# One decoder layer on one core: loads, tiles and transposes of the projection stage arranged in another way

## The chip, the core and the metric

The kernel runs on one core of a Trainium2 chip. Times are device microseconds (us) of one execution. The engines are PE (TensorE, matmuls and transposes), ACT (ScalarE), DVE (VectorE), POOL (GpSimd) and SP, which here only issues DMAs. Each engine runs its instructions in their order and waits on semaphores for the others.

## What is computed

One layer over 2048 tokens of width 1024, float32 in and out. The products are made in three parts of higher and lower halves, so that each float32 product of 128 tokens with a 1024 x 512 weight is 24 matmuls (3 terms, 8 blocks of k).

```python
a = _rmsnorm(h, g_in)                       # rows of x
q, k, v, gate_b, u_a, v_a, gate_a = split(a @ w_in)
q = _rope(_rmsnorm(q, q_norm), positions)   # 8 heads of 64
k = _rope(_rmsnorm(k, k_norm), positions)
o_b = _dilated_attention(q, k, v) * silu(gate_b)   # windows (128,1) (512,4) (2048,16)
o_a = _gmlp_spatial(u_a, v_a, w_spatial, b_spatial, ln_v_g, ln_v_b) * silu(gate_a)
h = h + concat(o_b, o_a) @ w_out
h = h + sigmoid(_rmsnorm(h, g_ple) @ w_ple_gate + b_ple_gate) * (p @ w_ple_proj)
```

## The kernel before

The work has three stages. In the first, 16 tiles of 128 tokens are scaled (`norm_T`, L206), turned so that the width lies on the partitions, and multiplied with the weights of gate_b (g), q, k and v (`project`, L227). A row tile is turned in one of two ways: the first `PE1` = 2 tiles by PE (`split_part`, L155), the others by the DMA (`turn_words`, L172): ACT takes the 32-bit words apart into two planes of 16 bits (L179), SP issues a DMA transpose for each (L181), DVE copies the planes back together (L183, two copies). `split_words` then makes the high part on ACT (L193) and the low part on DVE (L194), which PE reads as `aT`.

The four weights arrive in pieces of 256 KB on SP's queue (`load_group`, L127); ACT makes a high part (L133), Pool or DVE a low part (L135). The four small tables (positions `pos_i`, frequencies `freq`, `q_norm` and `k_norm` in `nrm`) and the broadcast of g_in to 128 partitions (`gbc`, L274, 512 KB) are loaded on SP's queue as well, gbc ahead of the weights and the others behind the first of them.

For each of q and k `post_qk` (L402) squares on ACT (L405), reduces (L407), rotates with tables `ta`, `tb` (L413, L415, sum on Pool L114), raises the sum of squares to the power -1/2 on Pool (L148, the scale before it on DVE L147), multiplies (L420) and splits in halves `hl` (ACT L422, DVE L423). `turn_qk` (L426) turns these with one DMA transpose `st<-hl` (L429), reorders k's result on ACT (L432) and stores it (L435). `post_gb` (L449) evacuates gate_b on ACT (L451) and DVE (L452) and stores it.

The loop over tiles has the order q, k, v, g of the tile before, while `prep(n)` makes the next one ready. A scheduler of the framework orders the instructions of each engine by priority in that loop; from attention on, PE's order is written out by hand (`in_order`). Buffers for pieces and turned words come from one ring of four, `stage()`, whose tiles are called raw.

In the second stage, attention works on 4 head pairs x 3 dilations in steps of four blocks; scores (L755) are followed after one step by the softmax (L758 to L766) and the splitting and turning of the probabilities (`Step.turn`, L769 to L781, `pt<-raw`), and after six steps by values (L791). gMLP products (L627) stand between as fill: `BLOCK0` = 18 units ahead of the first step, 1.3 per step after that. k and q of a head pair are loaded by `load_qk` (L257 to L266) into one set of buffers `sq` and `sk` by pieces, in the last steps of the pair before. The third stage (w_out, gate) has no part in the change.

## Time and profile before

| | |
|---|---|
| median of 3 runs | 1290.81 us (1289.02 to 1296.98) |
| the profiled execution | 1295.01 us, its span 1293.2 us |
| mean granted clock of PE | 0.976 |
| PE busy | 1201.3 us, 93% |
| DVE, ACT, POOL busy | 888.2, 648.9, 512.1 us |

PE is busy for nine tenths of the span, and the chain that ended last goes mostly through PE. Times in the profile are counted from the start of the span. An entry such as `[1.72 <-DVE gb L452]` behind a row says that the engine stood idle for 1.72 us before it and that DVE's instruction of line 452 on tile gb released it. A name such as `aT<-xt` is the tile written and the tile read. "x8" joins eight instructions that follow one another.

### The profile page before, as it was taken

Reading aid. Unit: us, or ns where it says so; the run is one execution under the profiler, and the core shown is the slowest. Engines: PE = TensorE matmul, PEld = TensorE weight load, DVE = VectorE, ACT = ScalarE, POOL = GpSimd, SP = SyncE. Lnnn points to the kernel's source line nnn. Section 1 sums busy time; section 2 is a strip of 40 time slices with the busy share of each in tenths; the row PEclk is TensorE's granted clock in tenths of the full one; section 3 lists DMA queues with packets and bytes.
Section 4 is the critical chain, followed back from the end, with each engine's and each line's share of the span. In section 5 each row is a group of like instructions: output and inputs, shape, how many; then the busy total and the mean of one; then the engine's idle time right before and its main releaser. Section 6 shows DMA issues by size and latency. Waiting matters only on the chain.

```text
span 1293.2 us, 21329 instructions
## 1 busy us (share of the span) xinstructions
PE 1201.3 (93%) x7166; PEld 976.0 (75%) x7166; DVE 888.2 (69%) x2253; ACT 648.9 (50%) x1273; POOL 512.1 (40%) x454
## 2 busy tenths in 40 slices
PE   5999999989995799899799799879999999999998
PEld 4778877767884687687687688768778888888887
DVE  5885565655575678778778678598766766666733
ACT  5754334334344577677677677444334434434422
POOL 4852343433453456555555565342212121221100
PEclk9999999999997899899999999989999999999999
DMA  7598777776769899999999999955555655654531
GB/s 263 160 229 197 168 183 166 165 180 157 175 171 239 202 202 220 219 216 236 218 217 223 219 229 215 207 176 174 141 147 123 165 156 128 153 162 127 143 90 49
DMA packets 442254, 233.21 MB, mean 180 GB/s; under 512 B 337440, under 2 KB 392864, under 8 KB 442144
## 3 DMA queue, kind: packets, MB, share of 16 engines
q1 hardware_dynamic: 442144, 231.85, 75.4%
q8 instruction: 56, 0.92, 0.3%
q14 instruction: 54, 0.44, 0.1%
HBM read 102.66 MB, written 57.28 MB: 124 GB/s over the span
## 4 chain that ended last, share of the span: by engine, by line
PE 41%; DMA 19%; DVE 16%; ACT 7%; issue 7%; POOL 6%; SPq 4%; DVEq 0%; ACTq 0%; POOLq 0%
PE mm L227 17%; PE mm L627 8%; PE gt L227 5%; DMA pt<-raw 4%; DMA xt<-raw 3%; PE s L227 3%; DMA st<-hl 3%; PE s L755 3%; PE pt L791 2%; DVE aT L194 2%; DMA ob<-d_o 2%; ACT raw L179 2%; POOL rsh L148 2%; DVE m L420 1%; DVE pr L758 1%
## 5 line engine op out<-in xcount | busy, mean ns | idle before, releaser
L227 PE MATMUL mm<-wslot,aT 128*128 128x512 f32 x1536 | 362.8, 392 | 7.8 <-ACT aT L193 3.3
L227 PEld LDWEIGHTS mm<-wslot,aT 128*128 128x128 f32 x1536 | 289.4, 189 | 70.4 <-ACT aT L193 4.6
L627 PE MATMUL mm<-wslot,aT 128*128 128x512 f32 x1152 | 317.9, 418 | 23.2 <-DVE raw L618 14.2
L627 PEld LDWEIGHTS mm<-wslot,aT 128*128 128x128 f32 x1152 | 214.1, 197 | 63.5 <-DVE raw L618 14.6
L114 POOL TENSOR_TENSOR raw<-pr,raw 128x512 f16<-128x512 f32 (+1 forms) x152 | 178.0, 1177 | 151.6 <-ACT raw L773 137.9
L766 ACT ACTIVATE pr<-pr,ost 128x256 f32<-128x256 f32 (+1 forms) x384 | 150.5, 451 | 78.8 <-DVE ost L764 70.9
L227 PE MATMUL gt<-wslot,aT 128*128 128x512 f32 x744 | 177.8, 393 | 6.1 <-DVE gb L452 5.3
L227 PEld LDWEIGHTS gt<-wslot,aT 128*128 128x128 f32 x744 | 139.8, 189 | 38.0 <-DVE gb L452 7.0
L791 PEld LDWEIGHTS <-pt 128*128 128x128 f16 x1800 | 66.3, 99 | 62.1 <-issue 33.7
L773 ACT ACTIVATE raw<-pr 128x512 f16<-128x512 f32 (+1 forms) x152 | 93.2, 620 | 39.6 <-DMA pt<-raw 37.4
L791 PE MATMUL pt<-sv,pt 128*128 128x65 f16 x1800 | 83.6, 196 | 21.8 <-DMA pt<-raw 21.8
L758 DVE CUSTOM_DVE_ANT_0 pr<-s,mask 128x256 f32<-128x256 f32 (+1 forms) x256 | 81.3, 359 | 29.7 <-POOL raw L114 16.0
L227 PE MATMUL av<-wslot,aT 128*128 128x512 f32 x360 | 86.0, 392 | 7.3 <-DVE gb L452 6.3
L227 PE MATMUL s<-wslot,aT 128*128 128x512 f32 x384 | 90.0, 390 | 1.6 <-POOL wslot L135 1.6
L114 POOL TENSOR_TENSOR m<-m,m 128x512 f32<-128x512 f32 x32 | 47.9, 1498 | 94.8 <-DVE rsh L147 88.8
L227 PEld LDWEIGHTS av<-wslot,aT 128*128 128x128 f32 x360 | 67.2, 188 | 23.6 <-DVE gb L452 7.9
L227 PEld LDWEIGHTS s<-wslot,aT 128*128 128x128 f32 x384 | 72.0, 188 | 17.0 <-POOL wslot L135 2.0
L755 PEld LDWEIGHTS <-sq 128*128 128x128 f16 x768 | 70.4, 121 | 13.7 <-issue 7.4
L755 PE MATMUL s<-sk,sq 128*128 128x256 f16 (+1 forms) x512 | 73.7, 279 | 7.0 <-DMA sk<-d_k 6.1
L566 POOL TENSOR_TENSOR ma<-ob,ma 128x512 f32<-128x512 f32 x16 | 24.5, 1533 | 122.1 <-DMA ma<-d_gb 58.0
L563 POOL TENSOR_TENSOR ob<-ob 128x512 f32<-128x512 f32 x16 | 21.0, 1314 | 126.5 <-DVE ob L561 126.5
L764 DVE TENSOR_SCALAR ost<-ost 128x2 f32<-128x2 f32 (+1 forms) x152 | 66.9, 442 | 2.6
(209 smaller groups left out, 1723.4 us busy)
## 6 DMA issues: line engine op xcount, KB each, us to landing
xt<-x SPq DMA_DIRECT2D x32, 512.0 KB, 4.6
d_o<-ost SPq DMA_DIRECT2D x48, 264.0 KB, 3.2
raw<-w_in SPq DMA_DIRECT2D x38, 256.0 KB, 3.7
sv<-d_vt SPq DMA_DIRECT2D x32, 264.0 KB, 3.5
ob<-d_o SPq DMA_DIRECT2D x16, 528.0 KB, 4.6
xt<-d_at SPq DMA_DIRECT2D x16, 512.0 KB, 5.0
out<-th SPq DMA_DIRECT2D x32, 256.0 KB, 2.8
d_at<-raw SPq DMA_DIRECT2D x28, 256.0 KB, 2.5
```

The source lines that it names most:

```text
L114: nc.gpsimd.tensor_tensor(dst, a, b, op=op)
L148: nc.gpsimd.tensor_tensor(dst, dst, mhalf[:, :width], op=OP.pow)
L179: nc.scalar.activation(turned[t].bitcast(U16), words[:, t], AF.Copy)
L194: nc.vector.tensor_tensor(lo, f, hi.bitcast(F32), op=OP.subtract)
L227: nc.tensor.matmul(ps, aT[:, ha, k, :], w(slot, hw, k), start=(n == 0), stop=(n == 3 * nk - 1))
L627: nc.tensor.matmul(ps, GT[c][:, ha, k, :], slots[g][:, hw, k, :], start=(n == 0), stop=(n == 23))
L755: nc.tensor.matmul(ps[:, c:c + nk], cols(br, j, Q[h]), cols(br, j, K, n, h, self.nb), start=(n == 0), stop=(n == 1))
L758: nc.vector.tensor_tensor_reduce(pr[:, c:c + nk], ps[:, c:c + nk], mask[:, m - nk:m], -1.0, 3e38, op0=OP.add, op1=OP.min, accum_out=o[:, j ...
L764: nc.vector.tensor_scalar(nm, nm, math.log(PSCALE), None, op0=OP.add)
L766: nc.scalar.activation(pr[:, c:c + nk], pr[:, c:c + nk], AF.Exp, bias=o[:, j - j0, 130 + h:131 + h], scale=-1.0)
L773: nc.scalar.activation(ph, pr[:, :width], AF.Copy)
L791: nc.tensor.matmul(PO[0][:, j % 2, h], self.pt[:, t, c // 128], vt[:, h, vv, 0:65], start=(n == 0), stop=(n == 3 * self.nb - 1))
```

## The change

1. g_in is read as two rows of 512 on ACT's queue; PE multiplies each by a column of ones into PSUM and DVE copies the result to `gbc`. The second tile's x is loaded on ACT's queue, too. The four small tables are loaded on Pool's queue; the rotation tables are computed behind the scaling of tiles 0 to 2.
2. `PE1` is 3: three tiles are turned by PE and each of the first weights meets three tiles. The order of weights is g, k, q, v.
3. In the loop k stands ahead of q. The copy back of the next tile's turned words, its splitting, its stores and the next x load (`finish(rest)`) get a place behind `LAST`, the two instructions that make q's halves of the current tile.
4. The spatial weights are prepared at tile 3 and parked in DRAM (`d_ws`); `gm_constants` loads them. `post_gb` of the last two tiles takes its buffer from `stage()`; gelu of c = 0 no longer does.
5. q and k lie in DRAM in blocks of 512 tokens, and `load_qk` loads a quarter of a head pair at a time, in four steps instead of three, k in two DMAs of 256 KB.
6. `BLOCK0` is 11. A step of width 256 has one DMA transpose and no longer two.

```diff
-BLOCK0, FILL = 18, 1.3
+BLOCK0, FILL = 11, 1.3
-PE1, PE3 = 2, 2
+PE1, PE3 = 3, 2
-        nc.sync.dma_start(gbc, bcast(io["g_in"], D))
-        ORDER = "gqkv"
+        XT[1] = stream.tile([128, D], F32, name="xt")
+        for i, t in enumerate((sn, cs)):
+            row = t.rearrange("p n d -> p (n d)")[0:1, :]
+            nc.scalar.dma_start(row, io["g_in"][0:1, 512 * i:512 * i + 512])
+            ps = bank("mm")
+            nc.tensor.matmul(ps, ones[0:1, :], row, start=True, stop=True)
+            nc.vector.tensor_copy(gbc[:, 512 * i:512 * i + 512], ps)
+        nc.scalar.dma_start(XT[1], x_t[1])
+        ORDER = "gkqv"
-        nc.sync.dma_start(pos_i, io["positions"].rearrange("o (n p) -> p (o n)", p=128))
+        nc.gpsimd.dma_start(pos_i, io["positions"].rearrange("o (n p) -> p (o n)", p=128))
...
-        for i in range(2):
-            nc.vector.tensor_copy(turned[i].bitcast(U16).rearrange("p (k c t) -> p t k c", t=2, k=nk),
-                                  halves[:, :, i * nk:i * nk + nk])
+        def back():
+            for i in range(2):
+                nc.vector.tensor_copy(turned[i].bitcast(U16).rearrange("p (k c t) -> p t k c", t=2, k=nk),
+                                      halves[:, :, i * nk:i * nk + nk])
+        if rest is None:
+            back()
+        else:
+            rest.append(back)
...
+            LAST[:] = [nc.scalar.activation(hl[:, :, 0], r, AF.Copy).ins,
+                       nc.vector.tensor_tensor(hl[:, :, 1], r, hl[:, :, 0], op=OP.subtract).ins]
...
-            g = p1g.tile([128, 512], F32, name="gb")
+            g = p1g.tile([128, 512], F32, name="gb") if n < NT - 2 else stage()
...
+        def finish(rest):
+            with tc.issue_after(LAST[0]), tc.issue_after(LAST[1]):
+                for f in rest:
+                    f()
...
-            t = pool.tile([128, 512], F32, name=name, bufs=n) if c else stage()
+            t = pool.tile([128, 512], F32, name=name, bufs=n)
...
+            if n < NT - 1:
+                for g in "kq":
+                    step(n - 1, g)
+            finish(rest)
+            if n < NT - 1:
+                for g in "vg":
+                    step(n - 1, g)
...
-            for t in range(2):
-                nc.sync.dma_start(qk[1][i:i + 64, t, :, tl], d_qk[1][64 * t:64 * t + 64, 2 * hp:2 * hp + 2, tl])
+            nc.sync.dma_start(qk[1][i:i + 64, c].rearrange("p t h s -> p t (h s)"),
+                              bass.AP(tensor=src.tensor, offset=src.offset,
+                                      ap=[[4 * HEADS * 512, 64], [64 * 4 * HEADS * 512, 2], [1, 1024]]))
...
-                        h, c = {10: (1, 0), 11: (1, 1), 0: (0, 2)}.get(i % 12, (4, 0))
+                        h, c = {10: (1, 0), 11: (1, 1), 0: (0, 2), 1: (0, 3)}.get(i % 12, (4, 0))
```

The lines below stand as the built programs have them. First ACT in one steady tile of the projection stage, before: sq of q and of k (from banks mm and s), the high part of the next tile (L193), both hl, gb, and behind them the square of the tile after (L210), k's reordering (L432) and the words (L179).

```order
L405 ACTIVATE sq<-mm 128x512
L179 ACTIVATE raw<-raw 128x256 x4
L193 ACTIVATE aT<-raw 128x512
L405 ACTIVATE sq<-s 128x512
L193 ACTIVATE aT<-raw 128x512
L422 ACTIVATE hl<-m_1536 128x8x64
L442 ACTIVATE vt<-av,sv 128x8x64
L422 ACTIVATE hl<-m_1581 128x8x64
L451 ACTIVATE gb<-gt 128x512
L210 ACTIVATE aT,ss<-xt 128x1024
L432 ACTIVATE hl<-st 128x1024
L179 ACTIVATE raw<-xt 128x1024 x2
```

The same engine and place in the changed kernel (s is k's bank there, mm q's; L456 is k's reordering, L202 the high part of the next tile, L475 gb):

```order
L429 ACTIVATE sq<-s 128x512
L183 ACTIVATE raw<-raw 128x256 x2
L429 ACTIVATE sq<-mm 128x512
L446 ACTIVATE hl<-m_1938 128x8x64
L466 ACTIVATE vt<-av,sv 128x8x64
L456 ACTIVATE hl<-st 128x1024
L446 ACTIVATE hl<-m_1984 128x8x64
L475 ACTIVATE gb<-gt 128x512
L202 ACTIVATE aT<-raw 128x512 x2
L183 ACTIVATE raw<-xt 128x1024
```

The high parts of the next tile have moved from among the squares to behind gb, and k's reordering from behind gb to ahead of q's halves. DVE at the same place of the changed kernel (L444 the multiplication, L447 the low half, L188 the copies back, L476 gb, L203 the low part of the next tile):

```order
L437 TENSOR_TENSOR m_1793<-mm,ta 128x512
L439 TENSOR_TENSOR m_1794<-mm,tb 128x8x32 x2
L150 TENSOR_SCALAR rsh<-ssh 128x8
L444 TENSOR_TENSOR m_1747<-m_1747,rsh 128x512
L447 TENSOR_TENSOR hl<-m_1747,hl 128x8x64
L467 SCALAR_TENSOR_TENSOR vt<-gt,sv,vt 128x8x64
L444 TENSOR_TENSOR m_1793<-m_1793,rsh 128x512
L447 TENSOR_TENSOR hl<-m_1793,hl 128x8x64
L188 COPY raw<-xt 128x2x512 x2
L188 COPY raw<-raw 128x2x128 x4
L476 SCALAR_TENSOR_TENSOR gb<-gb,av 128x512
L203 TENSOR_TENSOR aT<-raw,aT 128x512 x2
```

q's rotation stands ahead of k's multiplication, and the copies back follow q's low half, where before they stood ahead of the reduction of k. SP's queue where the projections end, in the changed kernel (mask, wsT, lng, lnb are gMLP's constants, sq and sk the first head pair's q and k):

```order
L471 DMA d_vp<-vt 32x4x1056
L485 DMA mask<-c_mask 128x512
L485 DMA wsT<-d_ws 128x512
L485 DMA lng<-ln_v_g 128x512
L485 DMA lnb<-ln_v_b 128x512
L477 DMA d_gb<-raw 128x512
L273 DMA sq_3482<-d_q 128x512
L130 DMA raw<-w_in 128x512 x2
L477 DMA d_gb<-raw 128x512
L130 DMA raw<-w_in 128x512
L273 DMA sq_3483<-d_q 128x512
L277 DMA sk<-d_k 64x2x1024 x2
```

The program's records say that the sq load in this piece waits for PE's last projection matmul. The same weight loads in the kernel before, for which the first head pair's q and k come later:

```order
L435 DMA d_k<-hl 1024x1x128
L127 DMA raw<-w_in 128x512 x4
L429 DMA_TRANSPOSE st<-hl 128x8x128
L127 DMA raw<-w_in 128x512 x2
L435 DMA d_q<-st 1024x1x128
L127 DMA raw<-w_in 128x512 x2
L429 DMA_TRANSPOSE st<-hl 128x8x128
L127 DMA raw<-w_in 128x512
L435 DMA d_q<-st 1024x1x128
L127 DMA raw<-w_in 128x512 x2
```

They stood between the transposes and stores of the last two tiles, and now stand behind these.

## Rows read from the trace of the kernel before

**Rows 1.** The page's first line: span and instructions of the profiled execution.

```profile
span 1293.2 us, 21329 instructions
```

**Rows 2.** PE's timeline 0 to 95 us; columns: start, length, engine, line, operation, [idle before, releaser].

```profile
9.70 1.97 PE L155 MATMUL pt<-ident,xt 128*128 128x128 f32 x8 [9.70 <-DVE xt L216]
...
22.75 0.49 PE L227 MATMUL mm<-wslot,aT 128*128 128x512 f32 x1 [2.96 <-ACT wslot L133]
...
90.88 4.47 PE L227 MATMUL mm<-wslot,aT 128*128 128x512 f32 x19
```

**Rows 3.** SP's queue (it issues the loads), timeline 0 to 32 us.

```profile
10.32 4.32 SPq L303 DMA_DIRECT2D freq<-c_freq  x1
...
15.71 0.83 SPq L127 DMA_DIRECT2D m<-w_in  x2
```

**Rows 4.** DVE's timeline, one row at the start and two in the projections of tiles 6 and 14.

```profile
8.36 1.29 DVE L216 SCALAR_TENSOR_TENSOR xt<-xt,rs,gbc 128x1024 f32<-128x1024 f32 x1 [2.75 <-DMA gbc<-g_in]
...
162.32 1.26 DVE L147 TENSOR_SCALAR rsh<-ssh 128x8 f32<-128x8 f32 x1
...
368.67 1.78 DVE L420 TENSOR_TENSOR m<-m,rsh 128x512 f32<-128x512 f32 x1 [2.93 <-POOL rsh L148]
```

**Rows 5.** Pool's timeline 0 to 32 us.

```profile
5.68 0.56 POOL L148 TENSOR_TENSOR rs<-rs,mhalf 128x1 f32<-128x1 f32 x1 [5.24 <-DVE rs L147]
```

**Rows 6.** PE's timeline in the projections of tiles 6 and 14.

```profile
168.92 5.78 PE L227 MATMUL av<-wslot,aT 128*128 128x512 f32 x24 [1.72 <-DVE gb L452]
...
344.35 11.04 PE L227 MATMUL mm<-wslot,aT 128*128 128x512 f32 x48
```

**Rows 7.** DVE's groups by form; columns: operation, count | busy, mean ns | idle before.

```profile
L420 DVE TENSOR_TENSOR m<-m,rsh 128x512 f32<-128x512 f32 x32 | 26.5, 830 | 12.7 <-POOL rsh L148 12.6
...
L423 DVE TENSOR_TENSOR hl<-m,hl 128x512 f16<-128x512 f32 x32 | 22.6, 705 | 9.1 <-ACT hl L422 9.1
...
L183 DVE COPY raw<-xt 128x1024 uint16<-128x1024 uint16 x28 | 19.6, 751 | 31.9 <-DMA xt<-raw 29.7 <-issue 2.2
...
L147 DVE TENSOR_SCALAR rsh<-ssh 128x8 f32<-128x8 f32 x32 | 20.3, 635 | 0.0
```

**Rows 8.** Pool's groups by form, same columns.

```profile
L148 POOL TENSOR_TENSOR rsh<-rsh,mhalf 128x8 f32<-128x8 f32 x32 | 59.6, 1864 | 1.0 <-DVE rsh L147 0.7
...
L114 POOL TENSOR_TENSOR m<-m,m 128x512 f32<-128x512 f32 x32 | 47.9, 1498 | 94.8 <-DVE rsh L147 88.8 <-DVE m L415 5.4 <-ACT hl L422 0.5
```

**Rows 9.** ACT's groups by form, same columns.

```profile
L422 ACT ACTIVATE hl<-m 128x512 f16<-128x512 f32 x32 | 20.1, 629 | 82.9 <-DVE m L420 82.9
...
L432 ACT ACTIVATE hl<-st 128x1024 f16<-128x1024 f16 x16 | 17.8, 1113 | 37.9 <-DMA st<-hl 35.3 <-DVE xt L216 2.6
```

**Rows 10.** DMA issues of the whole run: count, size, median us to landing.

```profile
raw<-w_in SPq DMA_DIRECT2D x38, 256.0 KB, 3.7
...
st<-hl SPq DMA_TRANSPOSE x32, 3.4
```

**Rows 11.** PE's timeline 340 to 450 us, from projections to attention.

```profile
387.87 11.04 PE L627 MATMUL mm<-wslot,aT 128*128 128x512 f32 x48
...
413.10 7.19 PE L627 MATMUL mm<-wslot,aT 128*128 128x512 f32 x24 [14.19 <-DVE raw L618]
...
424.41 0.40 PE L755 MATMUL av<-sk,sq 128*128 128x128 f16 x4
...
442.14 0.61 PE L791 MATMUL pt<-sv,pt 128*128 128x65 f16 x6 [5.84 <-DMA pt<-raw]
```

**Rows 12.** SP's queue, timeline 345 to 410 us.

```profile
349.46 2.73 SPq L127 DMA_DIRECT2D raw<-w_in  x2
```

**Rows 13.** Busy time by window: window, length, then busy us and count of each engine.

```profile
500.00:550.00 50.00, 42.76 (x378) 32.84 (x376) 38.34 (x128) 33.22 (x69) 30.31 (x27) 0.90 1.08 219
```

**Rows 14.** The page's costliest groups: scores in attention.

```profile
L755 PE MATMUL s<-sk,sq 128*128 128x256 f16 (+1 forms) x512 | 73.7, 279 | 7.0 <-DMA sk<-d_k 6.1
```

**Rows 15.** PE's timeline 853 to 876 us.

```profile
854.21 13.89 PE L627 MATMUL mm<-wslot,aT 128*128 128x512 f32 x48 [4.49 <-DVE gv L618]
```

More of the change, by code (lines that the diff above doesn't have):

```diff
@@ L92, in hybrid_layer @@
     dram = ctx.enter_context(tc.tile_pool(name="dram", bufs=1, space=bass.MemoryType.DRAM))
-    d_qk = [dram.tile([128, HEADS, S], F16, name=f"d_{n}") for n in "qk"]
+    d_qk = [dram.tile([128, 4, HEADS, 512], F16, name=f"d_{n}") for n in "qk"]
+    d_ws = dram.tile([128, 512], F32, name="d_ws")
     d_vp = dram.tile([S, HEADS * 132], F16, name="d_vp")
@@ L466, in spatial_weights @@
-        def spatial_weights():
-            wsT, gg, bs = pg.tile([128, 4, 128], F32, name="wsT"), CG["gg"], CG["bs"]
-            CG["wsT"] = wsT
-            keep = stage()[:, 0:128]
-            nc.vector.tensor_scalar(keep, CG["mask"][:, 384:512], 0.0, None, op0=OP.is_ge)
-            pt = bank("pt", (128, 4, 128))
+            for name, src in (("mask", io["c_mask"]), ("wsT", d_ws),
+                              ("lng", bcast(io["ln_v_g"], 512)), ("lnb", bcast(io["ln_v_b"], 512))):
+                CG[name] = pg.tile([128, 512], F32, name=name)
+                nc.sync.dma_start(CG[name], src)
@@ L481, in step @@
+                nc.tensor.transpose(ps[:, g], w, ident)
+            nc.vector.tensor_copy(gg, ps.rearrange("p g s -> p (g s)"))
+            nc.sync.dma_start(d_ws, gg)
+            nc.vector.tensor_scalar(bs, bs, 0.25, None, op0=OP.mult)
         def step(n, g):
@@ L489, in step, with prep, store @@
                 (post_v if g == "v" else post_gb)(n, ps)
-        def prep(n):
-            if n < NT:
-                xt = XT.pop(n)
-                turned = None if n < PE1 else (stage(), stage())
-                AT[n] = norm_T(xt, xt, p1g if n % 3 == 2 else stream, turned, gbc)
+        def prep(n, rest=None):
+            xt = XT.pop(n)
+            turned = None if n < PE1 else (stage(), stage())
+            AT[n] = norm_T(xt, xt, p1g if n % 3 == 2 else stream, turned, gbc, rest)
+            def store():
                 if turned is None:
@@ L507, in turn_p @@
             nc.sync.dma_start(pp, io["p"][0, 0][n * 128:(n + 1) * 128])
-            turn_words(pp, two(turned))
-            nc.sync.dma_start(d_p[n], turned)
-        prep(0)
-        prep(1)
+            turn_words(pp, two(turned), rest)
+            rest.append(lambda: nc.sync.dma_start(d_p[n], turned))
+        def finish(rest):
+            with tc.issue_after(LAST[0]), tc.issue_after(LAST[1]):
+                for f in rest:
+                    f()
+        for n in range(3):
+            prep(n)
+        with tc.issue_after(scaled[1].ins):
+            gA, gB = angles()
+        for n in range(3):
+            tables(n)
         for c, g in enumerate(ORDER):
```

241 lines of the change are left out of this document (122 added, 119 removed).

## The prediction

> **What bounds the kernel now.** I read the span first: 1293.2 us of profile in an execution of 1295.01 us, so 1.8 us lie around it, and that execution is 4.2 us above the median of the three timed runs, 1290.81 [rows 1]. The sum below is made against 1295.0 and the 4.2 us come off at its end. TensorE (PE) is the engine that ends last in almost every stage, so the time of the kernel is PE's work plus PE's waits, and I looked for the waits by PE's timeline, stage by stage.
>
> *Start.* PE's transposes of tile 0 end at 11.7 us, its first projection follows, and tile 3's first one runs at 90.88. In between PE waits 2.96 us at 22.75 for weights [rows 2], because the next weight load is issued only at 15.71: ahead of it stand the small tables, of which the issue of freq alone holds the queue for 4.32 us [rows 3]. VectorE (DVE) scales tile 0 at 8.36 after 2.75 us of waiting for gbc, the broadcast of g_in [rows 4].
>
> *Tiles 3 to 13.* A tile is four products of 24 matmuls. Where PE waits for nothing, from 344.35 to 387.87, it does eight such products, 5.44 us each, so a tile is 21.76 us of PE [rows 6, 11]. At 168.92 PE waits 1.72 us for gb, the evacuation of a g product; eight tiles show such a wait, from 0.67 to 2.24 us; this row is one of them. From 90.88 to 344.35 are 11 tiles: 253.5 us, against 11 x 21.76 = 239.4 us of work. So 14.1 us are lost there [rows 2, 6].
>
> *From projections to attention.* The last projection ends at 387.87. PE goes on with gMLP products at once, stands still for 14.19 us, begins scores at 424.41 and, after a further wait of 5.84 us, the first values at 442.14, 54.3 us after the last projection [rows 11]. The weight pieces for this (24 of 256 KB) were issued from 349.46 on, beside the last projections [rows 12].
>
> *Attention.* From 500 to 550 us PE is busy 42.76 of 50 [rows 13]; 600 to 650 and 700 to 750, each round a change of head pair like it, are two more of this kind. Waits of scores for k's loads add up to 6.1 us [rows 14]. Near the end of attention PE waits 4.49 us for gMLP values [rows 15].
>
> **The change, part by part.**
>
> *A, start: -4 us.* g_in now comes by two small rows, two matmuls and two DVE copies. That takes DVE's wait of 2.75 us away, but two copies of 512 columns (0.7 each, as DVE's passes of that size [rows 7]) come in front of the scaling: I take 1.2 us earlier, g's first matmul at 10.5. From there to tile 3 stand 12 products, 65.3 us, and the transposes of tiles 1 and 2, 1.97 each by tile 0's row [rows 2], 3.9. With 1.6 us for weights (before 2.96 and some small waits) the twelfth product ends at 81.3. But tile 3 is the first that goes through the DMA, and its transposes now stand on SP's queue behind tile 2's q transpose and v's stores: 3.4 for landing, 0.75 copy, 0.63 for its high part, and two issues of 0.42 ahead of it make 5.6 us [rows 3, 7, 9, 10], so tile 3 starts at 86.9 instead of 90.88. Bounds: -9.6 if v's last products cover the stall, and from above rival 5.
>
> *Pool's issues: nothing.* Four loads stand on Pool's (GpSimd's) queue ahead of the power that gives tile 0's scale, which runs at 5.68 [rows 5]. No row of before shows what an issue costs Pool. SP's take 0.42 each (two weight loads in 0.83) to 4.32 (freq) [rows 3]: four of them are 1.7 to 17.3 us. As Pool has nothing else to do before 5.68, the first costs nothing, the second delays all by some 12 us. I take nothing, since Pool's queue is empty there, where SP's had ten loads under way; the upper end is a rival. The Trainium skill (page "SBUF — State Buffer", section "SBUF: two separate sides") speaks against this part: a load issued from Pool has its descriptors written by GpSimd, which is locked out of the port it shares with VectorE while that engine runs certain copies. [...] No run so far shows a load from Pool; in the row above DVE waits until 8.36, so by the rule, too, four prompt issues are through before DVE's long work begins.
>
> *B, tiles 3 to 13: +11.6 us.* Now k's product comes first and the copy back of the next tile's turned words is put behind q's high and low parts. PE's wait for gb goes: g's first four matmuls run early in the tile and gb is only needed a tile later. What comes in its place? On ScalarE (ACT) the next tile's high part stands behind gb of this tile, and that behind q's high part, and that behind L456, the reordering of k, which waits for k's DMA transpose. I walk that chain from a tile's first matmul. k's 24 matmuls are done after 34 matmuls, 7.7 us; square 0.6 (an ACT pass like L422's); three DVE passes of 0.7, to 10.4; Pool's addition 1.50 and power 1.86, to 13.8. Meanwhile q is done after 52 matmuls, 11.8; square, three passes and the scale (0.6 + 2.1 + 0.64) keep DVE until 15.1, so k's last multiplication (0.83) ends at 16.0; high part 0.63, low part 0.71, 17.3; transpose 3.4, 20.7; L456 1.11, 21.8; q's high and low part, 23.1; first copy back 0.75, high part of the next tile 0.63: 24.5 [rows 7 to 10]. Passes that follow one another on an engine overlap by nearly 0.1 us (48 matmuls are listed with 11.04 us, and 192 took 43.52, which is 10.88 for 48 [rows 6, 11]), and I take 0.4 off: a tile is 24.1 us, a wait of 2.3 for PE. 11 x 24.1 = 265.1, against 253.5 before. From below: the last g matmul at 21.76, then gb and the high part, 0.63 each, gives 23.0, thus -0.5 in all. From above: the scale at 1.26 and one multiplication at 1.78, both seen in this stage [rows 4], give 1.6 more, 25.7, thus +29. I take the walk, because each of its steps is a mean of 14 rows or more.
>
> *C, transition: +2 us.* The two last gb tiles and the weight pieces share one ring of four buffers, and on SP's queue the first load of q, into a buffer that is free only when the last projection has been read, stands ahead of all 24 pieces. So the loads that ran beside the last projections now begin after them. Four pieces at a time, 3.7 to land, 0.63 for the high part and up to 1.5 for the low part where Pool makes it, are 1.45 us a piece [rows 8, 9, 10]: 35 us, scores at about 35 us after the last projection (36.5 before). gelu of c = 0 no longer waits for a ring buffer and the transposes of the first steps no longer stand behind loads, so values follow 17.7 - 5.8 = 11.9 us later, at 47 instead of 54.3 us [rows 11]. But PE will have done 84 gMLP matmuls by then, not 118 (BLOCK0 is 11 and no longer 18): 34 x 0.227 = 7.7 us that come later. -7.3 + 7.7 is about nothing; as q's and k's loads stand between the pieces, I take +2. Bounds: the landing alone, 0.9 us a piece, gives -11; 2.0 us a piece, with as much time again for q's, k's and v's loads in between, gives +15.
>
> *D, attention: -6 us.* k and q come in quarters, a step or two sooner, with runs of 2 KB and not of 1 KB. That should take the 6.1 us of waits for k [rows 14]. Upper end: all idle time of the three stretches, 3 x 7.2 = 22 us [rows 13]; lower end nothing, since the same bytes go over the same queue.
>
> *E, end of attention: -2 us.* The 7.7 us of gMLP work that come later (C) fill part of the wait of 4.49 [rows 15]; bounds 0 and -4.5. The single transpose for narrow steps, three tables instead of two and the parking of d_ws are off PE's path: nothing, or one transpose group of 1 us ahead of tile 3, which waits anyway.
>
> **Sum.** -4 + 11.6 + 2 - 6 - 2 = +1.6: 1296.6 in an execution like the profiled one, 1292.4 against the median; I say 1292.
>
> **Rivals.**
> 1. *k's chain is longer still (slower).* DVE's scale and multiplication at the slow values that they have beside Pool's work: 25.7 us a tile, 17.6 more in all than forecast, 1310. It decides from 25.2 us a tile on, which is 1304.5. For: Pool works for q while DVE multiplies for k. Against: the means already hold slow ones [rows 4, 7].
> 2. *The chain hides (the change does what its words say).* 23.0 us a tile: 12.1 less, 1280.3. For it: k now begins the tile, 4 us ahead of q. Against it: DVE takes q's passes first, until 15.1.
> 3. *Weights after the last projection (slower).* C at +15: 1305. For: all loads wait for one buffer, and the pieces share the queue with the loads of q, k and v. Against: the chip's queue lands a piece in 3.7 us also in this kernel's busy stages, of which that row is the median [rows 10].
> 4. *Attention gives all of its idle time back.* D at -22: 1276. For: in each of the three stretches PE's waits begin when the next pair's loads are on the queue. Against: most of these waits are for probabilities, not for k.
> 5. *Pool's issues are slow.* Up to 12 us, 1304.4. Under the skill's rule the same would follow for loads that DVE's work holds back.
>
> **Chances.** Forecast 0.42, with a range of its own from 1284 to 1301; longer chain 0.15; hidden chain 0.12; weights 0.10; attention 0.15; Pool 0.06. A measurement of this kernel can tell about 1% from no change, 13 us: under 1278 is faster, over 1304 slower. Slower: rival 1 (0.15), half of rivals 3 and 5 (0.08), and 0.06 of the forecast's upper tail, as each period error counts eleven times: 0.29. Faster: rival 4, half of 2 (with any gain from D or E above mine), and 0.02: 0.23. The same: 0.48. The range from 1274 to 1311 leaves out about one in ten at each end: attention beyond rival 4, and the bounds of B and C together.
>
> **What would show it.** B: in the profile after, PE's wait per tile at the first k matmul behind the high part of aT, about 2.3 us, a period of 24.1, and on ACT a wait of L456 for the transpose. If the wait is 1.2 and its releaser gb, rival 2 holds. A: tile 3's first matmul near 87, with a wait before it. C: w_in loads on SP only after the last projection, scores some 35 us later and values 47. D: no waits for k near a change of head pair. Pool: rs at 5.7 or later. The forecast fails if PE's wait per tile is off by more than a microsecond, since that counts eleven times.

## The result and the profile after

The changed kernel takes 1343.48 us in the median (1341.46 to 1347.15, 4 runs), the kernel before 1291.99 in the same comparison: a ratio of 1.0398, with a 95% interval from 1.0357 to 1.0438. It is slower by 51 us. The forecast was 1292, with a range up to 1311.

In the profiled execution the span is 1341.6 us against 1293.2. PE's timelines of these two executions, read at the same six marks, say where the 48.4 us lie:

| stretch | before | after | difference | forecast |
|---|---|---|---|---|
| to tile 3's first matmul | 90.9 | 105.5 | +14.7 | A: -4 |
| tiles 3 to 13 | 253.5 | 275.8 | +22.3 | B: +11.6 |
| tiles 14 and 15 | 43.7 | 45.5 | +1.8 | 0 |
| to the first values | 54.1 | 59.7 | +5.6 | C: -5.7 |
| attention, to the end of the last values | 388.4 | 383.7 | -4.7 | D: -6 |
| behind that | 462.7 | 471.4 | +8.6 | C's 7.7 of work that comes later, E: -2 |

The marks on PE's timeline after (columns as in [rows 2]; the first, third and later rows answer to [rows 2], [rows 6] and [rows 11]):

```profile
16.41 4.84 PE L239 MATMUL gt<-wslot,aT 128*128 128x512 f32 x11 [4.11 <-ACT aT L160]
...
97.75 0.93 PE L499 MATMUL pt<-ident,raw 128*128 128x128 f32 x4 [2.72 <-DVE raw L498]
105.53 2.07 PE L239 MATMUL s<-wslot,aT 128*128 128x512 f32 x4 [6.85 <-ACT aT L202]
...
156.38 1.27 PE L239 MATMUL s<-wslot,aT 128*128 128x512 f32 x4 [3.48 <-ACT aT L202]
157.45 1.91 PE L239 MATMUL mm<-wslot,aT 128*128 128x512 f32 x4
159.16 1.84 PE L239 MATMUL av<-wslot,aT 128*128 128x512 f32 x4
...
356.98 1.20 PE L239 MATMUL s<-wslot,aT 128*128 128x512 f32 x4 [3.23 <-ACT aT L202]
...
381.31 12.88 PE L239 MATMUL s<-wslot,aT 128*128 128x512 f32 x48 [2.26 <-ACT aT L202]
...
433.64 1.44 PE L675 MATMUL mm<-wslot,aT 128*128 128x512 f32 x2 [6.81 <-ACT wslot L136]
...
473.24 0.40 PE L804 MATMUL av<-sk,sq 128*128 128x128 f16 x4
...
486.50 0.36 PE L836 MATMUL pt<-sv,pt 128*128 128x65 f16 x6
```

g's first matmul is at 16.41, not at 11.56 as before or at 10.5 as forecast; PE stands still for 2.72 and 6.85 us ahead of tile 3; each tile from there on begins behind a wait for the high part of aT (3.48 at 156.38). After the last projection, which ends at 426.8, the gMLP matmul at 433.64 waits 6.81 us for a weight piece, scores begin 46.4 us and values 59.7 us after that end.

PE's waits, summed by line, of the changed kernel (columns: who waits for what, total us, times, longest):

```profile
PE s L239 <- ACT aT L202: 33.2, 12, 6.9
PE mm L675 <- ACT wslot L136: 25.6, 12, 6.8
```

The first row is A and B, the second C. Of the waits of scores for sk [rows 14] there is none left.

### The profile page after: what moved, and what is told of

Its sections match the earlier page's. It is cut to its first block, busy times and chain, and to the rows that moved or that the text cites. A ratio compares the mean times of both kernels' runs of the same rounds, so it can differ in the third digit from the quotient of the medians.

```text
span 1341.6 us, 21316 instructions
## 1 busy us (share of the span) xinstructions
PE 1219.9 (91%) x7178; PEld 983.7 (73%) x7178; DVE 864.9 (64%) x2253; ACT 654.5 (49%) x1273; POOL 514.5 (38%) x458
## 4 chain that ended last, share of the span: by engine, by line
PE 49%; DMA 20%; DVE 12%; ACT 6%; issue 5%; POOL 5%; SPq 3%; DVEq 0%; ACTq 0%; POOLq 0%
PE mm L239 20%; PE mm L675 8%; PE gt L239 7%; PE s L239 7%; DMA pt<-raw 5%; DMA raw<-w_in 4%; DMA st<-hl 3%; PE s L804 2%; PE pt L836 2%; PE av L239 2%; DVE pr L807 2%; DVE wslot L138 2%; DMA d_vp<-vt 2%; ACT pr L815 1%; PE av L804 1%
## 5 line engine op out<-in xcount | busy, mean ns | idle before, releaser
L239 PE MATMUL mm<-wslot,aT 128*128 128x512 f32 x1536 | 367.5, 393 | 4.6 <-DVE rsh L150 2.4
L675 PE MATMUL mm<-wslot,aT 128*128 128x512 f32 x1152 | 325.2, 422 | 33.8 <-ACT wslot L136 25.6
L815 ACT ACTIVATE pr<-pr,ost 128x256 f32<-128x256 f32 (+1 forms) x384 | 150.3, 451 | 63.9 <-DVE ost L813 60.2
L239 PE MATMUL s<-wslot,aT 128*128 128x512 f32 x384 | 98.6, 403 | 35.6 <-ACT aT L202 33.2
L836 PE MATMUL pt<-sv,pt 128*128 128x65 f16 x1800 | 82.2, 195 | 25.2 <-DMA pt<-raw 24.1
L239 PEld LDWEIGHTS av<-wslot,aT 128*128 128x128 f32 x360 | 69.1, 193 | 14.7
L151 POOL TENSOR_TENSOR rs<-rs,mhalf 128x1 f32<-128x1 f32 x32 | 20.2, 631 | 143.6 <-DVE rs L150 143.6
```

What stands on the lines that cost most here:

```text
L151: nc.gpsimd.tensor_tensor(dst, dst, mhalf[:, :width], op=OP.pow)
L239: nc.tensor.matmul(ps, aT[:, ha, k, :], w(slot, hw, k), start=(n == 0), stop=(n == 3 * nk - 1))
L675: nc.tensor.matmul(ps, GT[c][:, ha, k, :], slots[g][:, hw, k, :], start=(n == 0), stop=(n == 23))
L815: nc.scalar.activation(pr[:, c:c + nk], pr[:, c:c + nk], AF.Exp, bias=o[:, j - j0, 130 + h:131 + h], scale=-1.0)
L836: nc.tensor.matmul(PO[0][:, j % 2, h], self.pt[:, t, c // 128], vt[:, h, vv, 0:65], start=(n == 0), stop=(n == 3 * self.nb - 1))
```

## Experiments

The times below are medians, a ratio is that to the kernel before on the same chip, and stretches are read from one execution each. "The changed kernel" is at 1343.5.

### Four parts undone singly

**gb of the last two tiles in its own buffer** (a_gb_own)

```diff
-            g = p1g.tile([128, 512], F32, name="gb") if n < NT - 2 else stage()
+            g = p1g.tile([128, 512], F32, name="gb")
```

> The changed kernel with one line undone: gb of the last two tiles has its own buffer again and takes none of the ring of four. Theory R (ring): the weight pieces for gMLP were behind the end of the projections because gb of tiles 14 and 15 held two ring buffers whose release is the last projection; now the pieces load beside the last projections, scores begin 20 to 36 us after the last projection instead of 46.6, and the time falls by 12 to 25 us to 1318 to 1331. Rival Q (queue): q's first load, which waits for the last projection, or the splitting of the pieces sets it; scores stay at 44 to 48 us after the last projection and the time stays within 3 us of 1343.

Measured 1322.3 us, 21 less. The weight loads on SP's queue, first in the changed kernel, with q's first load and the second gb's store beside them, and then in this one:

```profile
426.85 0.33 SPq L273 DMA_DIRECT2D sq<-d_q  x1
427.22 0.96 SPq L130 DMA_DIRECT2D raw<-w_in  x2
428.29 0.54 SPq L477 DMA_DIRECT2D d_gb<-raw  x1
...
457.79 14.22 SPq L130 DMA_DIRECT2D raw<-w_in  x10
```

```profile
385.66 2.19 SPq L130 DMA_DIRECT2D raw<-w_in  x4
```

And what PE does at the end of the projections there:

```profile
422.85 11.04 PE L675 MATMUL mm<-wslot,aT 128*128 128x512 f32 x48
435.37 1.20 PE L675 MATMUL mm<-wslot,aT 128*128 128x512 f32 x4 [1.48 <-DVE gv L666]
445.43 0.59 PE L804 MATMUL av<-sk,sq 128*128 128x128 f16 x4 [8.86 <-DMA sv<-d_vp]
```

Scores begin 22.4 us after the last projection, not 46.4. So taking gb from the ring costs these 21 us: theory R holds. By which of two ways is less clear. The two ring buffers taken by gb are given back only with the last projection, and in the order that the scheduler made with that, q's first load, which waits for the last projection, stands ahead of all 24 pieces. The first two pieces go out before the second gb is stored, so for them it was the place in the queue that held; for the others the buffers may have held as well. This run takes both away: with the ring free the first pieces go out at 385.66, beside the projections, and PE goes on with gMLP at 422.85 without a wait. The same buffers with another order in the queue were not tried. What PE waits for now is sv, 8.86 us.

**The rest of a tile not put behind anything** (a_no_finish)

```diff
-            prep(n, rest)
+            prep(n)
...
```

> The changed kernel with the copy back, splitting, stores and next loads of a tile no longer put behind q's halves (finish is empty); order k, q and all else stay. Theory F (the placing): the 2.4 us wait per tile at the first k matmul goes, and with it the half clock behind it; the tile falls from 25.1 to 22.5 to 23.5 us, the time by 17 to 25 us, to 1318 to 1326. Rival O (order k before q, and the loads, set the tile): the tile stays at 24.5 to 25.5, the time within 5 us of 1343.

Measured 1327.1 us, 16.4 less, just beyond theory F's range. The wait at the first k matmul is gone and the old one for gb is back:

```profile
184.06 5.75 PE L239 MATMUL av<-wslot,aT 128*128 128x512 f32 x24 [1.54 <-DVE gb L476]
```

The last projection ends at 400.4 instead of 426.8, and as tile 3 starts at 103.7, a tile takes 23.0 us, as in the kernel before (253.5 / 11 = 23.0), with the order k, q in place. So the placing costs the tiles all of their 22 us, not the order. About 5 us of the gain go again at the transition: scores start 51.7 us after the last projection and not 46.4, as the pieces still wait there.

**k's reordering on Pool** (a_k_pool)

```diff
-                nc.scalar.activation(sp.rearrange("p h (r i) -> p h r i", r=4),
-                                     st.rearrange("p h (i r) -> p h r i", r=4), AF.Copy)
+                nc.gpsimd.tensor_copy(sp.rearrange("p h (r i) -> p h r i", r=4),
+                                      st.rearrange("p h (i r) -> p h r i", r=4))
```

> The changed kernel with the reordering of k (L456) made by Pool and no longer by ACT; the values are the same. Theory K (k's transpose stands in ACT's queue ahead of q's halves and the next high part): the wait per tile falls from 2.4 to 1.0 to 1.5 us, the tile from 25.1 to 23.2 to 24.2, the time by 10 to 20 us, to 1323 to 1333. Rival S (the copy back waits for its own transposes or for SP's queue): wait and tile stay, the time within 4 us of 1343.

Measured 1344.2 us: nothing. Theory K, which is the last part of the chain that the prediction walked, falls as the only cause. PE waits as long as in the changed kernel (1.65 to 3.92 us behind ten of the eleven tiles here, 1.33 to 3.48 behind all eleven there). In the changed kernel ACT does wait for k's transpose at this place (first fence, ACT's timeline); with the reordering on Pool, ACT (second fence) and DVE (third) wait for q's own chain, and it ends at the same time:

```profile
178.20 1.12 ACT L456 ACTIVATE hl<-st 128x1024 f16<-128x1024 f16 x1 [1.96 <-DMA st<-hl]
179.21 0.62 ACT L446 ACTIVATE hl<-m 128x512 f16<-128x512 f32 x1
180.08 0.60 ACT L475 ACTIVATE gb<-av 128x512 f32<-128x512 f32 x1 [0.25 <-PE av L239]
181.24 1.26 ACT L202 ACTIVATE aT<-raw 128x512 fp32r<-128x512 f32 x2 [0.56 <-DVE raw L188]
```

```profile
198.45 0.63 ACT L446 ACTIVATE hl<-m 128x512 f16<-128x512 f32 x1 [3.03 <-DVE m L444]
201.36 0.63 ACT L202 ACTIVATE aT<-raw 128x512 fp32r<-128x512 f32 x1 [2.28 <-DVE raw L188]
```

```profile
197.72 0.69 DVE L444 TENSOR_TENSOR m<-m,rsh 128x512 f32<-128x512 f32 x1 [1.30 <-POOL rsh L151]
199.11 1.57 DVE L447 TENSOR_TENSOR hl<-m,hl 128x512 f16<-128x512 f32 x1 [0.70 <-ACT hl L446]
200.60 1.35 DVE L188 COPY raw<-xt 128x1024 uint16<-128x1024 uint16 x2
```

q's multiplication starts at 197.72 behind Pool's power, its low half at 199.11, the copy back at 200.60, the high part at 201.36: 24.2 us after that tile's first matmul at 177.15. Two chains of about the same length lead to the copy back, one through k's transpose, one through q's arithmetic. This run shows that q's alone holds it; one that shortens q's alone was not made. The time is what rival S said, but what the copy back waits for here is q's low half, not its own transposes.

**The rest behind k's halves** (a_fin_k) asks the other way round, whether it is q's half that is too late a place:

```diff
-                for g in "kq":
-                    step(n - 1, g)
+                step(n - 1, "k")
+                behind_k = list(LAST)
+                step(n - 1, "q")
+                LAST[:] = behind_k
             finish(rest)
```

> The changed kernel with one thing moved: the copy back and the rest of the next tile are put behind k's halves and no longer behind q's. Theory H (q's half is what the copy back waits for, and k's half is there 4 to 5 us sooner): the wait per tile at the first k matmul goes to under 0.5 us, the tile from 25.1 to 21.8 to 22.6 us, the time by 22 to 35 us, to 1308 to 1321. Rival W (the words, their transposes and the x load on SP's queue set the tile): the tile stays above 24 us, the time above 1333.

Measured 1316.8 us, 26.7 less. PE in 50 us of this stage (columns as in [rows 13]; from 200 to 250 us it is the same):

```profile
150.00:200.00 50.00, 50.00 (x222) 41.44 (x221) 31.71 (x57) 24.70 (x40) 18.22 (x19) 1.00 0.84 200
```

PE (first pair of columns behind the length) is busy 50.00 of 50 us. No wait is left between tiles 4 and 15; a tile is 21.9 us, which is PE's work alone. Theory H holds, the idea of the change (put the turned tiles' work behind other work) is good, and the place one product further on is what costs. The last projection ends 37 us sooner than in the changed kernel; some 12 us of that are given back behind it: values come 63.9 us after the last projection and not 59.7, and attention and what follows take 4 us more each.

### The start

**All small tables on SP's queue** (a_tables_sp)

```diff
-        nc.gpsimd.dma_start(pos_i, io["positions"].rearrange("o (n p) -> p (o n)", p=128))
+        nc.sync.dma_start(pos_i, io["positions"].rearrange("o (n p) -> p (o n)", p=128))
```

and the same for freq and the two of nrm.

> The changed kernel with the four small tables on SP's queue again, at the place that they had before. Theory P (the element-wise load of positions runs on Pool's queue beside the first weight pieces and holds them up): g's first matmul moves from 16.4 to 11.5 to 13 us; 2 to 3 us of it come back at the second weight, as in the kernel before; the time falls by 1 to 5 us. Rival X (the second tile's x, now loaded first on ACT's queue, holds up the pieces): g's first matmul stays at 15.5 to 17, the time stays or grows by up to 4 us.

Measured 1329.7 us, 13.8 less, far more than either theory gave. g's first matmul is at 11.9. When ACT gets the third weight piece, in the changed kernel and then here:

```profile
13.30 0.63 ACT L136 ACTIVATE wslot<-vt 128x512 fp32r<-128x512 f32 x1 [3.73 <-DMA vt<-w_in]
```

```profile
8.94 0.61 ACT L136 ACTIVATE wslot<-vt 128x512 fp32r<-128x512 f32 x1
```

The DMA's share and rate in 8 to 12 and 12 to 16 us (last two columns), again first in the changed kernel:

```profile
8.00:12.00 4.00, 1.67 (x8) 1.57 (x8) 3.14 (x5) 1.46 (x3) 2.68 (x2) 1.00 0.89 77
12.00:16.00 4.00, 0.30 (x2) 0.00 (x0) 2.19 (x7) 2.58 (x5) 0.78 (x1) 1.00 1.01 387
```

```profile
8.00:12.00 4.00, 1.99 (x9) 1.69 (x9) 3.46 (x5) 3.88 (x9) 3.70 (x3) 1.00 1.01 275
12.00:16.00 4.00, 3.81 (x11) 2.72 (x11) 4.00 (x6) 1.35 (x3) 0.29 (x1) 1.00 0.07 15
```

In 8 to 12 us the engines of the DMA are about as busy in both (0.89 and 1.01), but move 77 GB/s while the small tables are under way beside the weights, and 275 without them. That is why g starts 4.5 us later. These 4.5 us do not last, though. On SP's queue the tables hold up the pieces behind them: the next one is issued at 12.53 us, the DMA moves 15 GB/s from 12 to 16 us, and PE waits for the second weight. First a later wait of the changed kernel, then two of this run:

```profile
74.10 7.32 PE L239 MATMUL mm<-wslot,aT 128*128 128x512 f32 x24 [2.44 <-DVE rsh L150]
```

```profile
19.30 0.80 PE L239 MATMUL s<-wslot,aT 128*128 128x512 f32 x1 [3.50 <-ACT wslot L136]
...
94.18 1.19 PE L239 MATMUL s<-wslot,aT 128*128 128x512 f32 x4 [3.11 <-ACT aT L202]
```

The 25th matmul of the projections starts at 25.27 us in the changed kernel and at 25.28 here, the 193rd at 68.68 and 69.04. Tile 3 starts 11.4 us sooner here, and that comes behind the 193rd: 4.3 us, nearly all from the wait of 2.44 us and the slow matmuls behind it (7.32 us for 24, 5.60 undisturbed), which this run does not have, and 7.4 ahead of tile 3, where PE's waits are 3.1 us here and 9.6 in the changed kernel. The order that the scheduler makes differs (tile 3's square stands earlier on ACT, at 74.9 instead of 86.6). So what the tables' place is worth came with that order and not from the first weights; why the scheduler orders it so stays open.

**Which table or which queue?** (a_pos_sp, a_pos_act, a_bc_act)

```diff
# a_pos_sp: positions alone on SP
-        nc.gpsimd.dma_start(pos_i, io["positions"].rearrange("o (n p) -> p (o n)", p=128))
+        nc.sync.dma_start(pos_i, io["positions"].rearrange("o (n p) -> p (o n)", p=128))
# a_pos_act: positions alone on ACT
-        nc.gpsimd.dma_start(pos_i, io["positions"].rearrange("o (n p) -> p (o n)", p=128))
+        nc.scalar.dma_start(pos_i, io["positions"].rearrange("o (n p) -> p (o n)", p=128))
# a_bc_act: positions on SP, the three broadcasts on ACT
-        nc.gpsimd.dma_start(freq, bcast(io["c_freq"], 32))
+        nc.scalar.dma_start(freq, bcast(io["c_freq"], 32))
```

> The changed kernel with only the load of positions on SP's queue again, behind the first weight group; the three other tables stay on Pool's. Theory P (the 2048 four-byte pieces of positions, and not the other tables, hold up the first weights): the third weight piece is split on ACT before 10 us instead of 13.3, g's first matmul comes at 11.5 to 13 instead of 16.4, the time falls by 4 us or more. Rival G (any load from Pool's queue does it, by its three broadcasts): the piece stays later than 12 us and g's first matmul later than 15.

> The changed kernel with only the load of positions on ACT's queue, behind the second tile's x; as ACT's order goes, tile 0's square then stands behind the first weight piece. Theory P (what matters is that the four-byte pieces run beside the first weights, on whatever queue): the rate of the loads from 8 to 12 us stays under 150 GB/s and the third weight piece is split at 12 us or later; the time stays within 6 us of 1343. Rival S (it is the software's queue of Pool that is slow): the rate is above 250 GB/s there, the piece is split before 10 us.

> The changed kernel with positions on SP's queue behind the first weight group and the three broadcast tables on ACT's queue, none on Pool's. Theory B (any small table that is moved in many small pieces beside the first weights holds them up, on whatever queue): the first weight piece is split at 9 us or later and g's first matmul comes at 15 us or later, the time stays above 1338. Rival P (it is Pool's queue): the first piece is split before 8 us and g's first matmul comes before 14 us; the time falls by 4 us or more.

Measured 1345.7, 1344.3 and 1338.9 us. When ACT splits the first and the third piece in a_pos_sp, in a_pos_act and in a_bc_act:

```profile
11.06 0.63 ACT L136 ACTIVATE wslot<-m 128x512 fp32r<-128x512 f32 x1 [5.49 <-DMA m<-w_in]
...
13.15 0.61 ACT L136 ACTIVATE wslot<-vt 128x512 fp32r<-128x512 f32 x1
```

```profile
8.96 0.63 ACT L136 ACTIVATE wslot<-m 128x512 fp32r<-128x512 f32 x1 [5.20 <-DMA m<-w_in]
...
13.79 0.63 ACT L136 ACTIVATE wslot<-vt 128x512 fp32r<-128x512 f32 x1
```

```profile
8.78 0.63 ACT L136 ACTIVATE wslot<-m 128x512 fp32r<-128x512 f32 x1 [2.73 <-DMA m<-w_in]
...
11.91 0.61 ACT L136 ACTIVATE wslot<-vt 128x512 fp32r<-128x512 f32 x1
```

With positions back on SP's queue and only the broadcasts on Pool's, the first piece is split even later (11.06 against 7.16), so theory P of that run (the four-byte pieces of positions alone) is wrong and rival G is right. In a_pos_act theory P's numbers came (78 GB/s in 8 to 12 us, the third piece at 13.79), but with three tables still on Pool's queue they prove nothing. With the broadcasts on ACT's queue the third piece is split at 11.91, later than the 8.94 with all tables behind the weights and sooner than 13.30; g's first matmul comes at 16.17 and the first piece at 8.78, a little sooner than theory B said. This speaks for the tables as such, beside the first weights, on either queue, but it is not a clean answer: ACT's order changed with it (the square of tile 0 stands behind the first piece there), which may delay g by itself. What stands is that the four tables, issued behind the first eight weight pieces, leave them alone, and that each of the three ways to start some of them at once delays the third by 3 to 5 us. In all three PE still waits 8.4 to 9.3 us ahead of tile 3, so no single table brings about that part.

### q and k by 512 tokens, alone

**The kernel before with this part only** (b_qk512): the blocks of 512 in DRAM, `load_qk` by quarters, one transpose for narrow steps.

```diff
-                        h, c = {10: (1, 0), 11: (1, 1), 0: (0, 2)}.get(i % 12, (4, 0))
-                        loads = load_qk(qk, hp + h, c, 1 + c // 2) if i > 1 and hp + h < 4 else iter(())
+                        h, c = {10: (1, 0), 11: (1, 1), 0: (0, 2), 1: (0, 3)}.get(i % 12, (4, 0))
+                        loads = load_qk(qk, hp + h, c) if i > 1 and hp + h < 4 else iter(())
```

> The kernel before with q and k by 512 tokens and the single transpose for narrow steps, and nothing else of the change. Theory D (the waits of scores for k's loads go): 6.1 us of waits fall to under 1.5, the time falls by 3 to 8 us to 1283 to 1288. Rival N (the bytes are the same and the queue is as full; probabilities' transposes wait instead): waits of values for their transposes grow by what the others lose, the time stays within 2 us of 1291.

Measured 1281.2 us, a ratio of 0.9903 (0.9869 to 0.9937): 12.6 us faster than before, more than theory D said. Scores and values in its groups by form:

```profile
L760 PE MATMUL s<-sk,sq 128*128 128x256 f16 (+1 forms) x512 | 72.6, 278 | 0.0
...
L792 PE MATMUL pt<-sv,pt 128*128 128x65 f16 x1800 | 81.8, 194 | 26.3 <-DMA pt<-raw 25.5 <-DVE gv L647 0.5
```

The waits for sk are gone (7.0 to 0.0), and those of values for their transposes grow from 21.8 to 26.3 (the groups of before: 7.0 and 21.8), so rival N is half right: what k no longer holds up waits in part for the next thing. Attention from first to last values still shortens from 388.4 to 380.7 us, and the first values come 5 us earlier, of which 2.6 are there at the end of the projections. The blocks of 512 and the single transpose were not tried apart. In the changed kernel attention is 4.7 us shorter, with all parts of the change in it.

### Parts together

**Three parts undone** (a_three: gb's buffer, tables on SP, nothing put behind) and **the same with the rest behind k's halves** (a_three_k)

> The changed kernel with three parts undone together: gb of the last two tiles in its own buffer, small tables on SP's queue, nothing put behind q's halves. Theory A (the three losses lie in different stages and add up): 1343.5 - 21 - 16 - 14 = 1292, between 1288 and 1297, no different from the kernel before. Rival B (they share a loss, above all the wait before tile 3 and the weight loads): 1300 to 1310.

> The changed kernel with gb of the last two tiles in its own buffer, small tables on SP's queue, and the next tile's rest behind k's halves. Theory H: tiles of 21.8 to 22.6 us, thus 5 to 15 us less than the same with nothing put behind: 1278 to 1288, faster than the kernel before. Rival W: tiles above 24 us, 1305 or more.

Measured 1290.9 and 1271.8 us (0.9988, 0.9964 to 1.0012; and 0.9833, 0.9800 to 0.9866). The three losses of 21.2, 16.4 and 13.8 us add up to 51.3 of the 52.6 us that a_three wins: each shows in another stretch first, and they add. Theory A of a_three and theory H of a_three_k hold (the latter with 6 us more than it said). With these three parts undone what is left of the change (order k, q, the quarters and the rest) stands where the kernel before does. The rest of a tile put behind k's halves is worth another 19 us.

**Two tiles for the first weights, and BLOCK0** (a_three_k_two, a_three_k_b18, both together a_three_k_two_b18)

```diff
-PE1, PE3 = 3, 2
+PE1, PE3 = 2, 2
-BLOCK0, FILL = 11, 1.3
+BLOCK0, FILL = 18, 1.3
```

In a_three_k_two the loops over the first tiles run to PE1 as well.

> The fastest version so far (gb in its own buffer, tables on SP's queue, the rest behind k's halves) with two tiles turned by PE and met by the first weights instead of three. Theory T (three tiles per weight cover the loads): two tiles wait for weights once more per group, tile 3 starts 3 to 8 us later than 94.4, the time grows by 3 to 8 us from 1271.8. Rival E (the first weights are in time for two tiles; the third tile's turn on PE and the wait before tile 3 eat what three tiles give): tile 3 starts within 2 us of 94.4 or sooner, the time stays within 2 us or falls.

> The fastest version so far with BLOCK0 18, as before the change. Theory M (gMLP work at the front only moves: what is not done there is done behind attention): scores come 6 to 7 us later, the stretch behind attention is shorter by as much, the time stays within 3 us of 1271.8. Rival V (the front has room, PE waits there for k, q and v anyway): scores come less than 3 us later and the time falls by 3 to 7 us.

> The fastest version so far (1260.2, BLOCK0 18) with two tiles for the first weights instead of three. Theory A (the two gains of 7 and 11.7 us lie in different stages): 1250 to 1256. Rival S (both fill the same room ahead of attention): 1258 to 1262.

Measured 1264.9, 1260.2 and 1260.8 us. Two tiles instead of three are 7 us faster, as rival E allows: PE stands still for 1.05 us ahead of the first tile that comes through the DMA and not for 3.09, and the last projection ends at 378.2 instead of 380.9. The other 4 us of the 7 lie behind the projections and were not followed. BLOCK0 18 is 11.7 us faster, more than either side said. PE at the end of the projections with it:

```profile
378.82 16.85 PE L677 MATMUL mm<-wslot,aT 128*128 128x512 f32 x72
...
396.32 2.07 PE L677 MATMUL mm<-wslot,aT 128*128 128x512 f32 x8
398.23 0.40 PE L806 MATMUL av<-sk,sq 128*128 128x128 f16 x4
```

80 gMLP matmuls now stand where 52 stood, and scores begin at the same 19.3 us after the last projection: the front had the room, for in a_three_k PE waits there 6.64 us for v. Of the 15.8 us between the two profiled executions 10.2 lie behind attention (464.1 us against 474.4 in a_three_k), where less gMLP work is left to do. Both gains together are no more than the larger one, so rival S of that run holds; why was not followed. a_three_k_b18 is at 0.9746 (0.9722 to 0.9769) of the kernel before: 33 us faster than it and 83 faster than the change.

## Why the prediction was wrong, step by step

**Pool's issues.** The failed step of A is "Pool's issues: nothing": a_tables_sp, which undoes it, takes 13.8 us back. The bound that it weighed, the time of an issue on Pool, was asked and answered rightly: the four take 1.37, 0.57, 0.54 and 0.54 us, and the power runs at 5.78, in [rows 5] at 5.68.

```profile
1.27 1.37 POOL L325 DMA_DIRECT2D pos_i<-positions  x1 [0.82 <-POOLq L992]
...
3.72 0.54 POOL L330 DMA_DIRECT2D nrm<-k_norm  x1
5.78 0.57 POOL L151 TENSOR_TENSOR rs<-rs,mhalf 128x1 f32<-128x1 f32 x1 [1.52 <-DVE rs L150]
```

The question that was not asked is what these transfers do to the others. They land after 7.3 to 9.4 us and the third weight piece is split 4.4 us late (13.30 against 8.94). [rows 3] could have warned: I read the 4.32 us of freq's issue as the cost of standing in a full queue, and did not ask how long such a transfer, of 128 rows of a few bytes, occupies the path. But that is not what the 13.8 us are: on SP's queue the same tables cost PE as much until the 25th matmul. They came with another order of the work ahead of tile 3, of which the prediction had no term. The rule of the Trainium skill that I weighed there (page "SBUF — State Buffer", section "SBUF: two separate sides") did not come into play: no run here shows DVE holding up a load of Pool's, as all four are issued by 4.3 us and DVE is idle from 1.04 to 5.54.

**The rest of A.** Tile 3 starts 18.6 us later than forecast. 5.9 of them are there at g's first matmul (16.41, not 10.5). 7.8 come while the first weights meet three tiles, 78.6 us and not 70.8: the sum had 1.6 us of waits, and PE waits 0.49, 2.40, 0.66 and 2.44 us and runs slow matmuls at the start and behind the last of these waits. 4.9 come ahead of tile 3, where I had 5.6 us: PE's waits are 9.6 (2.72 and 6.85), with a short transposition of the spatial weights between them. The sum had the right items there, but on ACT tile 3's own square stands at 86.64, behind q's halves of the first tiles, and its words at 94.67, when v's products are nearly done; its transposes are issued at 98.45. In a_tables_sp, where the square stands earlier, 3.1 us are left, in a_three_k_two 1.05.

**B.** The chain was walked to a wait of 2.3 us for PE. The eleven waits measured are 1.33 to 3.48, 2.4 in the mean. The wait and its size were right, and so were the steps of the walk: in tiles 4 to 12 hl of k begins 15.4 to 17.0 us after the tile's start (I said 16.0), k's transpose has landed at 20.2 to 21.8 (20.7). What failed is the term 21.76 for PE's own work: a tile takes 25.07 us, of which 22.67 are PE at work. So the sign that I had named, a wait off by more than a microsecond, did not come, and the forecast failed all the same. Behind some of the waits PE runs at its lower clock for a few microseconds. In the fence at the top groups of four matmuls take 1.91 and 1.84 us at 157.45 and 159.16, against 1.08 undisturbed. The granted clock there, and behind the wait of 3.23 us at 356.98 (third column from the end):

```profile
148.00:152.00 4.00, 4.00 (x19) 3.34 (x18) 2.27 (x3) 1.09 (x2) 3.37 (x3) 1.00 0.36 68
...
156.00:160.00 4.00, 3.62 (x10) 2.84 (x11) 2.85 (x8) 2.05 (x4) 0.00 (x0) 0.67 0.96 233
...
160.00:164.00 4.00, 4.00 (x17) 3.29 (x16) 0.27 (x2) 2.06 (x3) 0.55 (x1) 0.90 1.10 325
...
356.00:360.00 4.00, 3.02 (x13) 2.51 (x14) 3.46 (x9) 1.86 (x3) 0.00 (x0) 1.00 1.06 241
```

1.00 before the wait, 0.67 and 0.90 after it: part of the stretch is at 1.2 GHz instead of 2.4. Behind 3.23 us it is 1.00. The mean of 0.9 us a tile hides two kinds of tile: in four of the eleven (those that begin at 105.53, 156.38, 255.52 and 306.12, behind waits of 6.85, 3.48, 2.71 and 2.94 us) PE is at work for 23.7 to 24.0 us, in the other seven for 22.06. So the lower clock cost 6.7 us in four tiles, and 3.3 are 0.3 us a tile beside the wait; together they are 10.0 of the 10.7 us by which B was too small. The 1.8 us of tiles 14 and 15 are again the lower clock, behind a wait of 2.26 us (48 matmuls in 12.88 us, not 11.04). The length of the wait alone does not decide it, as 2.76 and 3.23 us were followed by the full clock and 2.26 was not; what does was not followed. In the kernel before, eight shorter waits add up to 11.6 of the 14.1 us lost in this stage [rows 2, 6], 0.3 us each beside their own length, and none was followed by slow matmuls; I had put the price of a wait at its length.

As to the cause, k's transpose was named as what binds. a_k_pool shows that q's arithmetic holds the copy back as long, a_fin_k that the place behind q's halves explains all of the wait.

**C.** The sum had 1.45 us a piece. Measured are 24 pieces from 427.22 to about 472, 1.87 us each: q's, k's and v's loads stand between them, which was the bound of 2.0 that I put at +15 and made rival 3. The measured C is +5.6, and with the 7.7 us of later work, taken as forecast, +13.3. The mechanism was in the text, and the choice of the value was wrong: I argued from the landing of one piece, not from what shares the queue. The prediction also named q's first load as what stands ahead of the pieces; it does stand there, and a_gb_own shows that it goes from there when the ring is free.

**D and E.** -4.7 and about +0.9 (8.6 less C's 7.7) against -6 and -2. The waits for sk went as forecast, all of them (8.4 us with both groups of scores, 6.1 of it named in the sum). But the values' waits, mostly for their transposes, grew from 21.8 to 25.2 us in attention and took 3.4 back; that leaves 5.0, which is about what attention gained. Behind attention 204 gMLP matmuls stand and not 163, some 7 us more of PE's work, and the waits there add up to 13.8 us as against 13.6: the later work filled none of them.

Of the 51 us against a forecast of nothing, 18.6 lie in A, 10.7 in B, 1.8 behind it, 11.3 in C and 4.2 in D and E, together 46.6. But for rounding that is the 48.4 us of the two spans less the 1.6 that were forecast. Rivals 1, 3 and 5 named the stages, though A's loss came by another way than slow issues on Pool and most of B's excess by the clock; each was priced alone, and what came were losses in three stages at once.

## What to carry to other kernels

- Work that is to hide behind other work has to be placed by its own deadline: here the next tile's high part is needed 21.8 us after a tile starts, what is put behind q's halves begins at 23.3 to 24.9, and what is put behind k's halves is there in time. A tile took 25.1 us with the one, 21.9 with the other and 23.0 with nothing put behind.
- A short wait of PE that comes back in a loop can cost more than its length: here the lower clock added 1.6 to 1.8 us behind four of the eleven waits between tiles. Give it a term with a bound of its own.
- A buffer taken from a shared ring can hold up whatever loads use the ring next, by itself or by the order that is made around it. When a tile is moved to another pool, look for the loads that queue behind its release.
- Ask of every early transfer what it does to those beside it and behind it, and follow a delay to the end of the stage: 4.5 us at the first matmul were made up by the 25th, and what lasted came from the order made with the transfer's new place.

## What the runs showed of the hardware

- With 88 KB of small tables, moved as broadcasts and single elements, beside the first weights the DMA's rate in 8 to 12 us was 77 GB/s and not 275, while its engines stayed nearly as busy (0.89 against 1.01). With the same tables on SP's queue it was 15 GB/s in 12 to 16 us, at a share of 0.07. An issue on Pool's queue took 0.54 to 1.37 us.
- Behind a wait of 3.48 us PE's granted clock was 0.67 and 0.90 in the next two stretches of 4 us; behind one of 3.23 us it was 1.00.
